# An encoder layer in fp32 on one core: attention's side work in other slots, the gate/up stage opened in another order, the last columns staggered

## The chip, the cores and the metric

The kernel runs on one core of a Trainium2 chip. The core has a matrix engine (TensorE, PE in the profile), a vector engine (VectorE, DVE), a scalar engine (ScalarE, ACT), a general engine (GpSimd, POOL) and a sync engine (SyncE, SP), which here issues the transfers. Each engine works through its own queue in order. The metric is device time of one launch in microseconds; less is better.

## The reference

One layer of an encoder on a 2048 x 1024 fp32 sequence: three kinds of mixing side by side, an output projection, and a gated feed-forward block.

```python
h = ada_norm(x, norm1_g, sh1, sc1)
proj = h @ w_in
y_na   = neighbourhood_attention(q, k, v, rpb)          # 4 heads, 2-D windows
y_mla  = latent_attention(c_q, c_kv, k_rope, ...)       # 8 heads, all 2048 keys
y_conv = short_conv(x_in, gate_b, gate_c, conv_w, conv_b)
mixed = concatenate([y_na, y_mla, y_conv], -1)
mixed = rms_norm(mixed in groups of 64, out_norm_g)
x = x + g1 * (mixed @ w_out)
h2 = ada_norm(x, norm2_g, sh2, sc2)
gt, up = split(h2 @ w_gu)                               # 1024 -> 2 x 2816
x = x + g2 * ((silu(gt) * up) @ w_down)                 # 2816 -> 1024
```

## The kernel before, in words

All arithmetic is fp32. A product is made of three passes over rounded halves (high x high, high x low, low x high; helper `three`), so each operand is split into a high part (a copy on ScalarE, `whl` or `put`) and a low part (a subtraction on VectorE). Work runs on 128-partition tiles and chunks of 512 tokens (CH).

**Latent attention** (lines 1030 to 1290) has 32 units, `mla`: 8 heads, each with 4 query chunks (qc). A unit has 8 key pairs, done two at a time: the loop steps through kp = 0, 2, 4, 6, and n counts key pairs over all units. For a key pair TensorE makes scores (L1198 to L1200), ScalarE the exponentials, GpSimd and VectorE add them into two running sums `acc` (L1212, L1213), and TensorE multiplies by the values (L1147), two key pairs later. The PE, ACT, DVE and POOL orders of this part are those of the code, since it stands in a hand-ordered section; SP's order is made by the scheduler. What is left of a unit is done in the slots of the next one:

- `finish` copies the result out of PSUM (L1155), and a DMA brings its upper half beside the lower (`o<-o`, L1157). `join` (L1159 to L1163) adds the halves on GpSimd (L1162) and stores them to `mixT`. It stands at kp = 2.
- `sums` closes the running sum in five stages, at kp = 0, 2, 2, 4, 4: GpSimd adds the two sums (L1175); ScalarE rounds the result (`ah`, L1178); GpSimd makes the rest (`al`, L1181); TensorE sums both over partitions with a vector of ones (L1184, L1185); ScalarE squares, and SP stores to `s2d` (L1188, L1189). For the last unit the first three stages are left out, and TensorE sums `acc` itself in full fp32 (L1173).
- `put_max` sends the next unit's row of maxima to its query tile (`qh<-mr`, L1141), which its first score product reads.
- `load_head` loads the next head's keys, queries and values, in the first unit of a head.
- `wd_combos` (L1034 to L1056) prepares differences of blocks of w_down: loads of four blocks (`wt`, L1044), four subtractions on GpSimd (L1054), each stored (`wdt`, L1056). It is a generator, stepped once each time n is a multiple of 4, five steps per set of blocks.

In attention's last units `mix_in(0)` prepares the first chunk for the projection, one step per call.

**Output projection** (`out_proj`, four chunks, two halves each): eight slices of w_out, each split by L1320 (ACT) and L1321 (DVE), then 12 matmuls (L1420 to L1422). Its `side` is a list of generators that are stepped once for each slice. Results are multiplied by a gate (L1455), added to x on GpSimd (L1456) and stored to `x1d` (L1428); in the last two chunks x is held in the four `xs` buffers.

**Gate and up.** A fast matrix product with seven products in place of eight, on 2 x 2 blocks: token blocks A11, A12, A22 and sums S1 to S4, against weight blocks B11 to B22 and sums T1 to T4 (made by L1346 on GpSimd from raw loads `draw`, L1334). `gate_set` does seven products of 12 matmuls (L1601 to L1603) in the order A11, S2, A12, S3, S1, A22, S4, and copies or adds their results (L1608 to L1629). `gate_up` runs one set for the gate, then one for up, for each of 11 column blocks f and each of two pairs of token chunks p. `first_early` and `first_late` make the token operands of the first pair (`put`, L1523 and L1524): `first_late` all of S3, S1, A22, S4 ahead of the first gate set. A22 takes the place of h1, which is why its four tiles are copied to `xs` buffers first (L1549). A list of units with a look-ahead of four gives the order in which weights are split; loads run up to three ahead.

**Down** (`down`): seven products over 11 slices of 2 x 512 rows, four token tiles each in its own PSUM bank; results go through VectorE (L1695, L1701) and GpSimd (L1703) to `out`. From `out_proj` on, PE and SP are in the order of the code; ACT, DVE and POOL by the scheduler.

## Time and profile before

| what | value |
|---|---|
| three runs | 3131.87, 3136.46, 3139.70 us (median 3136.46) |
| profiled execution | 3138.71 us, of it span 3136.9 us |
| PE busy | 2958.9 us (94%), mean granted clock 0.976 |
| VectorE, ScalarE, GpSimd busy | 2031.2, 1300.0, 1377.5 us |
| latent attention, 32 units | about 770 to 1558 us |
| output projection | 1566 to 1774 us |
| gate and up, down (first pair) | 1774 to 2487 us |
| gate and up, down (second pair) | 2487 to 3137 us |

In the rows below a line of the timeline holds the start, the length, the engine, the line of the code, the operation, output<-input by the program's names and shapes, and in brackets how long the engine sat idle before it and what released it. "x4" is four such instructions in a row, with the length of all. PEclk is the granted clock of TensorE, 1.00 being 2.4 GHz; its other level is half of that. A matmul's length is longer than its share of the engine's time, since matmuls overlap: at full clock one of 512 columns begins 0.23 us after the one ahead of it.

### The profile page before, as it was taken

Reading aid. Unit: us, or ns where it says so; the run is one execution under the profiler, and the core shown is the slowest. Engines: PE = TensorE matmul, PEld = TensorE weight load, DVE = VectorE, ACT = ScalarE, POOL = GpSimd, SP = SyncE. Lnnn points to the kernel's source line nnn. Section 1 sums busy time; section 2 is a strip of 40 time slices with the busy share of each in tenths; the row PEclk is TensorE's granted clock in tenths of the full one; section 3 lists DMA queues with packets and bytes.
Section 4 is the critical chain, followed back from the end, with each engine's and each line's share of the span. In section 5 each row is a group of like instructions: output and inputs, shape, how many; then the busy total and the mean of one; then the engine's idle time right before and its main releaser. Section 6 shows DMA issues by size and latency. Waiting matters only on the chain.

```text
span 3136.9 us, 38944 instructions
## 1 busy us (share of the span) xinstructions
PE 2958.9 (94%) x13554; PEld 2225.1 (71%) x13554; DVE 2031.2 (65%) x2892; ACT 1300.0 (41%) x2298; POOL 1377.5 (44%) x1011
## 2 busy tenths in 40 slices
PE   6988999889999999999999789999999899999998
PEld 5877788756555555555477567888777788888886
DVE  7778684646766676667666765665677655555556
ACT  4544454465433343334535433333354333333443
POOL 4433333432566666566645654445212344443002
PEclk9999999989999999999999899999999999999999
DMA  6566555786233322330255334333466633333565
GB/s 217 168 228 217 197 191 155 225 192 170 74 94 95 89 75 62 94 88 29 73 185 185 118 97 128 124 124 111 135 221 222 195 101 101 102 107 102 195 233 193
DMA packets 329575, 448.05 MB, mean 143 GB/s; under 512 B 39625, under 2 KB 178169, under 8 KB 326297
## 3 DMA queue, kind: packets, MB, share of 16 engines
q1 hardware_dynamic: 329378, 445.56, 46.0%
q8 instruction: 107, 1.75, 0.2%
q14 instruction: 90, 0.74, 0.1%
HBM read 323.70 MB, written 117.51 MB: 141 GB/s over the span
## 4 chain that ended last, share of the span: by engine, by line
PE 66%; DMA 11%; DVE 11%; issue 5%; POOL 3%; ACT 2%; SPq 1%; POOLq 0%; ACTq 0%; DVEq 0%
PE bk L1601 8%; PE bk L1603 8%; PE bk L1602 8%; PE op L1147 7%; PE ps L846 4%; PE bk L1421 3%; PE bk L1420 3%; PE bk L1422 3%; PE st L1198 3%; PE st L1199 3%; PE st L1200 3%; DVE whl L1321 2%; PE mm L316 2%; PE mm L320 2%; PE mm L321 2%
## 5 line engine op out<-in xcount | busy, mean ns | idle before, releaser
L847 DVE TENSOR_REDUCE mx<-ps 128x1 f32<-128x1024 f32 x256 | 313.0, 1223 | 251.6 <-PE ps L846 248.9
L1205 ACT ACTIVATE p<-st 128x1024 f32<-128x1024 f32 x256 | 261.8, 1023 | 405.9 <-PE st L1200 389.3
L1321 DVE TENSOR_TENSOR whl<-draw,whl 128x512 fp32r<-128x512 f32 x372 | 282.3, 792 | 183.7 <-ACT whl L1320 183.1
L1320 ACT ACTIVATE whl<-draw 128x512 fp32r<-128x512 f32 x372 | 219.3, 625 | 314.0 <-PE bk L1422 193.2
L1212 POOL TENSOR_TENSOR acc<-acc,p 128x512 f32<-128x512 f32 x192 | 256.6, 1336 | 122.7 <-ACT p L1205 118.9
L1421 PE MATMUL bk<-whl 128*128 128x512 f32 x616 | 243.5, 395 | 20.2 <-DVE whl L1321 20.2
L1147 PE MATMUL op<-p,vt 128*64 128x512 f32 x1024 | 253.5, 616 | 0.1
L1346 POOL TENSOR_TENSOR t<-draw 128x512 f32<-128x512 f32 x88 | 124.3, 1413 | 273.1 <-DMA draw<-in_w_gu 209.2
L1422 PE MATMUL bk<-whl 128*128 128x512 f32 x616 | 241.0, 391 | 0.0
L1420 PE MATMUL bk<-whl 128*128 128x512 f32 x616 | 240.8, 391 | 0.0
L1601 PE MATMUL bk<-q,whl 128*128 128x512 f32 x528 | 210.7, 399 | 24.5 <-ACT ev L1608 16.2
L1360 ACT ACTIVATE whl<-t 128x512 fp32r<-128x512 f32 x176 | 110.9, 631 | 274.8 <-PE bk L1603 238.5
L1361 DVE TENSOR_TENSOR whl<-t,whl 128x512 fp32r<-128x512 f32 x176 | 171.2, 974 | 62.8 <-ACT whl L1360 58.3
L1602 PE MATMUL bk<-q,whl 128*128 128x512 f32 x528 | 208.6, 395 | 0.0
L1603 PE MATMUL bk<-q,whl 128*128 128x512 f32 x528 | 207.7, 393 | 0.0
L1198 PE MATMUL st<-qh,kh 97*128 97x512 f32 x512 | 207.2, 405 | 0.0
L1199 PE MATMUL st<-ql,kh 96*128 96x512 f32 x512 | 204.1, 399 | 0.0
L1200 PE MATMUL st<-qh,kl 96*128 96x512 f32 x512 | 203.1, 397 | 0.0
L262 POOL TENSOR_TENSOR wlo<-raw,whi 128x768 fp32r<-128x768 f32 (+4 forms) x59 | 111.7, 1893 | 194.9 <-ACT whi L261 174.8
L1213 DVE TENSOR_TENSOR acc<-acc,p 128x512 f32<-128x512 f32 x192 | 193.1, 1006 | 4.3 <-ACT p L1205 4.2
L846 PE MATMUL ps<-kh,qh 96*128 96x512 f32 x512 | 179.2, 432 | 3.9 <-DMA kh<-krh 2.1
L320 PE MATMUL mm<-whi,hh 128*128 128x288 f32 (+3 forms) x512 | 171.4, 346 | 8.3 <-ACT hh L384 4.9
(353 smaller groups left out, 7269.0 us busy)
## 6 DMA issues: line engine op xcount, KB each, us to landing
draw<-in_w_gu SPq DMA_DIRECT2D x176, 256.0 KB
draw<-actd SPq DMA_DIRECT2D x70, 512.0 KB
actd<-xs SPq DMA_DIRECT2D x88, 256.0 KB
draw<-wdt SPq DMA_DIRECT2D x40, 512.0 KB
actd<-ev SPq DMA_DIRECT2D x66, 256.0 KB
wt<-in_w_adat SPq DMA_DIRECT2D x32, 512.0 KB
draw<-in_w_out SPq DMA_DIRECT2D x32, 512.0 KB
draw<-in_w_down SPq DMA_DIRECT2D x30, 512.0 KB
```

The costliest lines, as they stand in the source:

```text
L846: pe.matmul(ps[:, e], qs, kh[:QKD, kc:kc + CH], start=True, stop=True)
L847: v.reduce_max(mx[:, t, i:i + 1], ps.rearrange("p a b -> p (a b)"), axis=AX.X)
L1147: pe.matmul(tl["op"][e * HD:(e + 1) * HD], vt[:, 2 * kp + e], tl["p"][kp][:, e], start=kp == 0, stop=kp == NP - 1, skip_group_check=True)
L1198: pe.matmul(st[:, e], kh[:, ks], qh[:, qsl], start=True, stop=False)
L1199: pe.matmul(st[:, e], kh[:QKD, ks], ql[:, qsl], start=False, stop=False)
L1321: v.tensor_tensor(out=w[:, 1], in0=raw[:, e], in1=w[:, 0].bitcast(F32), op=ALU.subtract)
L1420: pe.matmul(ps, th, wh, start=first, stop=False, skip_group_check=True)
L1421: pe.matmul(ps, th, wl, start=False, stop=False, skip_group_check=True)
L1422: pe.matmul(ps, tl, wh, start=False, stop=last, skip_group_check=True)
L1601: pe.matmul(ps, w[:, 0, k], th, start=first and k == 0, stop=False, skip_group_check=True)
L1602: pe.matmul(ps, w[:, 0, k], tl, start=False, stop=False, skip_group_check=True)
L1603: pe.matmul(ps, w[:, 1, k], th, start=False, stop=k == KH - 1, skip_group_check=True)
```

## The change

Seven edits:

1. `join` goes from kp = 2 to kp = 4; in GpSimd's order it then stands behind `al` and two more additions.
2. `wd_combos` is stepped at kp = 4 and kp = 6 of every unit from n = 16 on, and its first yield of each set is gone, so a set takes four steps. It ends some six units earlier.
3. `mix_in(0)` gets one more step at the start of the last unit but one.
4. The last unit's sums leave attention: `last_sums` does them as a side generator of `out_proj(0)`, after its first two slices have been issued. `acp` moves to another pool group so that `acc` lives on.
5. For the first column block of the first pair the products go: gate A11, S2, A12; up A11, S2, A12; then the other four of gate, and the other four of up. The list of weight units follows, `first_late` becomes a generator that is stepped in between, and its copies to `xs` move from VectorE to ScalarE. The second half of the norm (`norm2_later`) starts with the second block, f = 1.
6. In `down`, for the last output block, `u2` is multiplied by the gate and added to x before its last product, so that only the product itself is multiplied and added behind it. Of these last additions GpSimd does those of token tiles 0 and 2, VectorE those of 1 and 3.
7. In the second pair's last product the last two slices are done token tile by token tile.

```diff
 wd_combos:
             for k in range(NFF // 2):
-                yield
                 if k + 1 < NFF // 2:
...
-                if n >= 16 and n % 4 == 0:
+                if n >= 16 and kp >= 4:
                     next(combos, None)
-                if prev and kp == 2:
+                if prev and kp == 4:
                     join(prev, state[prev])
...
+                if ui == len(mla) - 2 and kp == 0:
+                    next(side)
...
+            if f or p:
+                for u in range(2):
+                    item(2, partial(gate_load, f, u), gate_prep, 7)
+            else:
+                for u in range(2):
+                    item(2, partial(gate_load, f, u), gate_prep, 0)
+                i = len(stream) - 2
+                units.extend((i + u, e) for es in (range(3), range(3, 7)) for u in range(2) for e in es)
...
+    def last_sums(acc, u):
+        yield
+        sp = bank()
+        for e in range(2):
+            pe.matmul(sp[:1], ones_f[:, 0:1], acc[:, e], start=e == 0, stop=e == 1)
+        t = tmp()
+        s.activation(t[:1], sp[:1], AF.Square, scale=math.sqrt(EPS))
+        dma(s2d[u[0]:u[0] + 1, u[1] * CH:(u[1] + 1) * CH], t[:1])
...
 first_late:
             put(S, "S3", k, t)
+            yield
...
-            v.tensor_copy(t, h1[:, KH + k])
+            s.activation(t, h1[:, KH + k], AF.Copy)
...
 gate_up:
-        gate_set(S, gate, side)
+        sets = [gate_set(S, gate, side, f + p == 0), gate_set(S, up, side, f + p == 0)]
+        if f + p == 0:
+            next(sets[0])
+            next(sets[1])
+            drain(early)
+        for _ in sets[0]:
+            pass
         stores()
-        gate_set(S, up, side)
+        for _ in sets[1]:
+            pass
...
 down, prod:
+                if end and k == NK - 2:
+                    held = a, w
+                    continue
+                ks = ((k - 1, *held), (k, a, w)) if end and k == NK - 1 else ((k, a, w),)
...
+                        if (i, j) == (0, 1):
+                            v.tensor_tensor(out=u2[t], in0=u2[t], in1=g2b[:, CH:], op=ALU.mult)
+                            g.tensor_tensor(out=xx, in0=xx, in1=u2[t], op=ALU.add)
...
-        prod(c, False, (0, 1))
-        add(u2, u2, c)
-        put_out(0, 1, u2)
+        prod(c, False, (0, 1), p == PAIRS - 1)
+        put_out(0, 1, c)
```

The lines of the changed kernel have other numbers: L1175, L1181, L1162, L1212 and L1054 become L1170, L1176, L1161, L1207 and L1053; L1334 and L1428 become L1332 and L1432; L1695 and L1701 become L1734 and L1740, L1703 becomes L1742.

GpSimd's order around one end of a unit in attention: `acc` are the score sums and, in the row with one input, the close of the unit's sum; `o` is `join`, `al` the rest of the rounded sum, `wt` a weight sum. Before:

```order
L1212 TENSOR_TENSOR acc<-acc,p_9184 128x512
L1175 TENSOR_TENSOR acc<-acc 128x512
L1212 TENSOR_TENSOR acc<-p_9195,p_9222 128x512
L1212 TENSOR_TENSOR acc<-acc,p_9238 128x512
L1162 TENSOR_TENSOR o_9209<-o_9209,o 64x512
L1181 TENSOR_TENSOR al<-acc,ah 128x512
L1212 TENSOR_TENSOR acc<-acc,p_9264 128x512
L1212 TENSOR_TENSOR acc<-acc,p_9284 128x512
L1054 TENSOR_TENSOR wt<-wt 128x512
```

And after:

```order
L1207 TENSOR_TENSOR acc<-acc,p_8840 128x512
L1170 TENSOR_TENSOR acc<-acc 128x512
L1207 TENSOR_TENSOR acc<-p_8853,p_8880 128x512
L1207 TENSOR_TENSOR acc<-acc,p_8892 128x512
L1176 TENSOR_TENSOR al<-acc,ah 128x512
L1207 TENSOR_TENSOR acc<-acc,p_8918 128x512
L1207 TENSOR_TENSOR acc<-acc,p_8936 128x512
L1053 TENSOR_TENSOR wt<-wt 128x512
L1161 TENSOR_TENSOR o_8867<-o_8867,o 64x512
```

`join` has moved from ahead of `al` to three operations behind it, past a weight sum.

SP's order at the opening of the gate stage: `draw<-in_w_gu` are gate and up weights (four loads make one column block of gate or up), `x1d<-xs` the last stores of the projection, `n<-x1d` loads for the norm, `actd` stores of the first block's results. Before:

```order
L1428 DMA x1d<-xs 128x512 x4
L1446 DMA xs<-in_x 128x512 x4
L1334 DMA draw<-in_w_gu 128x4x128 x8
L1495 DMA n_15653<-x1d 128x512
L1428 DMA x1d<-xs 128x512 x4
L1428 DMA h2d<-n_15736 128x4x128
L1334 DMA draw<-in_w_gu 128x4x128 x4
L1495 DMA n_15807<-x1d 128x512
```

And after:

```order
L1432 DMA x1d<-xs 128x512 x4
L1460 DMA xs<-in_x 128x512 x4
L1332 DMA draw<-in_w_gu 128x4x128 x12
L1432 DMA x1d<-xs 128x512 x4
L1332 DMA draw<-in_w_gu 128x4x128 x4
L1509 DMA n_15936<-x1d 128x512
L1432 DMA actd<-ev 128x512 x2
```

Twelve weight loads stand ahead of the last `x1d` stores, where eight stood, and the norm's first load comes behind them.

VectorE's last operations: `u` are the four token tiles of the last output block, `bk` their PSUM banks, `g2b` the gate, `xs` the tiles that are stored. Before:

```order
L1695 TENSOR_TENSOR u_23928<-u_23928,bk 128x512
L1695 TENSOR_TENSOR u_23929<-u_23929,bk 128x512
L1701 TENSOR_TENSOR u_23928<-u_23928,g2b 128x512
L1695 TENSOR_TENSOR u_23930<-u_23930,bk 128x512
L1701 TENSOR_TENSOR u_23929<-u_23929,g2b 128x512
L1695 TENSOR_TENSOR u_23931<-u_23931,bk 128x512
L1701 TENSOR_TENSOR u_23930<-u_23930,g2b 128x512
L1701 TENSOR_TENSOR u_23931<-u_23931,g2b 128x512
```

And after:

```order
L1740 TENSOR_TENSOR u_23932<-bk,g2b 128x512
L1740 TENSOR_TENSOR u_23933<-bk,g2b 128x512
L1742 TENSOR_TENSOR xs<-xs,u_23933 128x512
L1740 TENSOR_TENSOR u_23934<-bk,g2b 128x512
L1740 TENSOR_TENSOR u_23935<-bk,g2b 128x512
L1742 TENSOR_TENSOR xs<-xs,u_23935 128x512
```

The four additions from PSUM are gone, the multiplication reads PSUM itself, and two sums with x are now here.

## Rows read from the trace of the kernel before

**Rows 1.** The page's chain that ended last, shares by engine.

```profile
PE 66%; DMA 11%; DVE 11%; issue 5%; POOL 3%; ACT 2%; SPq 1%; POOLq 0%; ACTq 0%; DVEq 0%
```

**Rows 2.** PE's waits: what waited, for whom, us in total, times, longest.

```profile
PE bk L1601 <- ACT ev L1608: 16.2, 1, 16.2
...
PE mi L1185 <- POOL al L1181: 15.1, 6, 2.8
...
PE bk L1601 <- DVE ev L1618: 6.0, 1, 6.0
PE bk L1420 <- ACT whl L1320: 5.6, 2, 3.9
```

**Rows 3.** Windows of a head's first unit, its second, and six heads.

```profile
core 0: us, PE busy (x) PEld busy (x) DVE busy (x) ACT busy (x) POOL busy (x), PEclk, DMA share, GB/s
864.01:891.71 27.70, 25.50 (x100) 14.38 (x99) 17.38 (x19) 9.81 (x11) 15.93 (x12) 0.94 0.85 188
891.71:915.47 23.76, 23.76 (x100) 13.91 (x99) 16.49 (x19) 9.69 (x11) 15.15 (x11) 1.00 0.08 25
864.01:1461.18 597.17, 582.03 (x2378) 337.48 (x2377) 404.28 (x410) 233.34 (x264) 375.21 (x278) 0.98 0.32 80
```

**Rows 4.** Timeline of POOL in those two units.

```profile
881.02 1.27 POOL L1162 TENSOR_TENSOR o<-o,o 64x512 f32<-64x512 f32 x1 [7.14 <-DMA o<-o]
882.26 1.78 POOL L1181 TENSOR_TENSOR al<-acc,ah 128x512 fp32r<-128x512 f32 x1
...
905.16 1.27 POOL L1181 TENSOR_TENSOR al<-acc,ah 128x512 fp32r<-128x512 f32 x1 [1.88 <-ACT ah L1178]
```

**Rows 5.** Timeline of SP, ACT and PE at that head change.

```profile
868.65 0.49 SPq L1157 DMA_DIRECT2D o<-o  x1
...
876.76 0.62 ACT L1178 ACTIVATE ah<-acc 128x512 fp32r<-128x512 f32 x1
...
884.09 0.40 PE L1185 MATMUL mi<-al,ones_r 128*1 128x512 f32 x1 [2.20 <-POOL al L1181]
```

**Rows 6.** Timeline from attention to the projection: SP, PE, ACT, PE.

```profile
1554.86 0.90 SPq L1069 DMA_DIRECT2D m<-mixT  x2
...
1555.42 2.22 PE L1147 MATMUL op<-p,vt 128*64 128x512 f32 x8
...
1562.36 2.17 ACT L1090 ACTIVATE t<-m 128x512 f32<-128x512 f32 x4
...
1566.15 0.79 PE L1420 MATMUL bk<-whl,th 128*128 128x512 f32 x1 [3.94 <-ACT whl L1320]
```

**Rows 7.** Window of the first gate/up block, same columns as rows 3.

```profile
1774.50:1850.30 75.80, 47.62 (x177) 36.42 (x177) 59.45 (x57) 30.77 (x57) 62.45 (x41) 0.82 0.25 74
```

**Rows 8.** Timeline of SP, POOL and ACT in that block.

```profile
1785.96 11.49 SPq L1428 DMA_DIRECT2D x1d<-xs  x4
...
1793.72 3.38 POOL L1456 TENSOR_TENSOR xs<-xs,eg 128x512 f32<-128x512 f32 x2
...
1797.89 0.60 ACT L1608 ACTIVATE ev<-bk 128x512 f32<-128x512 f32 x1
...
1812.34 6.75 POOL L1555 TENSOR_TENSOR ev<-ev,tl 128x512 f32<-128x512 f32 x4
```

**Rows 9.** Timeline of DVE near attention's end, one operation.

```profile
1543.82 3.70 DVE L1124 TENSOR_TENSOR tl<-t,th 128x512 fp32r<-128x512 f32 x1 [0.98 <-ACT th L1123]
```

**Rows 10.** Timeline of DVE in the second pair's down stage.

```profile
2978.30 1.29 DVE L1321 TENSOR_TENSOR whl<-draw,whl 128x512 fp32r<-128x512 f32 x2 [1.43 <-ACT whl L1320]
```

**Rows 11.** Timeline of PE at the second pair's first gate block.

```profile
2491.29 0.79 PE L1601 MATMUL bk<-m,whl 128*128 128x512 f32 x1 [4.26 <-DVE ev L1612]
```

**Rows 12.** Timeline of the end: PE, DVE, POOL.

```profile
3126.87 0.39 PE L1422 MATMUL bk<-whl 128*128 128x512 f32 x1
...
3129.69 2.03 DVE L1701 TENSOR_TENSOR u<-u,g2b 128x512 f32<-128x512 f32 x2
...
3131.25 2.81 POOL L1703 TENSOR_TENSOR xs<-xs,u 128x512 f32<-128x512 f32 x2 [0.68 <-DVE u L1701]
```

**Rows 13.** Timeline of SP at the head change: one weight load.

```profile
873.83 7.92 SPq L1044 DMA_DIRECT2D wt<-in_w_down  x1
```

More of the change, by code (lines that the diff above doesn't have):

```diff
@@ L1006, in encoder_trunk @@
         egp = c5.enter_context(tc.tile_pool(name="egp", bufs=2, reuse_waits="tile"))
+        acp = c5.enter_context(tc.tile_pool(name="acp", bufs=2, reuse_waits="tile"))
         pw = mk("pw", 6)
-        acp = mk("acp", 2)
         ms = mk("ms", 1)
@@ L1167, in sums @@
             acc = tl["acc"]
-            if u == mla[-1] and stage < 3:
+            if u == mla[-1]:
                 pass
-            elif u == mla[-1] and stage == 3:
-                tl["sp"] = pmi.tile([P, CH], F32, name="mi")
-                for e in range(2):
-                    pe.matmul(tl["sp"][:1], ones_f[:, 0:1], acc[:, e], start=e == 0, stop=e == 1)
             elif stage == 0:
@@ L1274, in encoder_trunk @@
                             if stage == 4:
+                                last_acc = state[prev]["acc"]
                                 del state[prev]
@@ L1377, in encoder_trunk @@
         for f in range(NK):
-            for u in range(2):
-                item(2, partial(gate_load, f, u), gate_prep, 7)
+            if f or p:
[6 more added lines that the diff above has]
+                units.extend((i + u, e) for es in (range(3), range(3, 7)) for u in range(2) for e in es)
         for op, name in zip(LEFT, ORDER):
@@ L1541, in first_late @@
             put(S, "S3", k, t)
+            yield
+        a22, s4 = [], []
+        s2 = hi_lo(S, "S2").bitcast(F32)
         for k in range(KH):
@@ L1545, in first_late @@
             put(S, "S1", k, t)
-        a22, s4 = [], []
-        for k in range(KH):
             t = xsp.tile([P, CH], F32, name="xs")
-            v.tensor_copy(t, h1[:, KH + k])
+            s.activation(t, h1[:, KH + k], AF.Copy)
             a22.append(t)
-        s2 = hi_lo(S, "S2").bitcast(F32)
-        for k in range(KH):
             t = ev.tile([P, CH], F32, name="ev")
@@ L1556, in first_late @@
             s4.append(t)
+            yield
         for k in range(KH):
             put(S, "A22", k, a22[k])
+            if k % 2:
+                yield
         for k in range(KH):
             put(S, "S4", k, s4[k])
+            if k % 2:
+                yield
     def operands(p, S):
@@ L1591, in operands, with gate_set @@
                 yield
-    def gate_set(S, after, side):
+    def gate_set(S, after, side, lead):
         def prod(ps, op, first):
@@ L1606, in gate_set @@
         prod(a, "A11", True)
+        if lead:
+            step(side, 2)
         p1 = ev.tile([P, CH], F32, name="ev")
@@ L1612, in gate_set @@
         v.tensor_tensor(out=u2, in0=p1, in1=b, op=ALU.add)
-        step(side)
+        step(side, 2 if lead else 1)
         prod(a, "A12", False)
         after(0, 0, a)
+        if lead:
+            step(side, 2)
+        yield
         prod(b, "S3", False)
@@ L1675, in down, with prod @@
         xs = []
-        def prod(ps, first, at=None):
+        def prod(ps, first, at=None, end=False):
             for k in range(NK):
                 a, w = unit_next(), unit_next()
+                if end and k == NK - 2:
+                    held = a, w
+                    continue
+                ks = ((k - 1, *held), (k, a, w)) if end and k == NK - 1 else ((k, a, w),)
                 for t in range(NTT):
                     sl = slice(t * P, (t + 1) * P)
-                    three(ps[t], a[:, 0, sl], a[:, 1, sl], w[:, 0], w[:, 1], first and k == 0, k == NK - 1)
+                    for kk, a, w in ks:
+                        three(ps[t], a[:, 0, sl], a[:, 1, sl], w[:, 0], w[:, 1], first and kk == 0, kk == NK - 1)
                 if k == 4:
@@ L1699, in put_out @@
             for t in range(NTT):
-                e = u3[t] if src is a else src[t]
+                e = u3[t] if src is a else u2[t] if src is c else src[t]
                 v.tensor_tensor(out=e, in0=src[t], in1=gb, op=ALU.mult)
                 xx = xs.pop(0)
-                g.tensor_tensor(out=xx, in0=xx, in1=e, op=ALU.add)
+                (v if src is c and t % 2 else g).tensor_tensor(out=xx, in0=xx, in1=e, op=ALU.add)
                 pending.append((out[tokens(2 * p + i, t), j * CH:(j + 1) * CH], xx))
+        c = None
         a = four()
@@ L1738, in encoder_trunk @@
         x1a = block("q0").rearrange("p (t h) n -> p t (h n)", h=2)
-        out_proj(0, mTs[0], [mix(1)], x1a)
+        out_proj(0, mTs[0], [last_sums(last_acc, mla[-1]), mix(1)], x1a)
         x1b = block("q1").rearrange("p (t h) n -> p t (h n)", h=2)
@@ L1753, in encoder_trunk @@
                     side = [norm2_later()]
-                    first_late(S, h0, h1)
+                    early = [first_late(S, h0, h1)]
                 for f in range(NK):
-                    gate_up(p, f, S, side)
+                    gate_up(p, f, S, early if f + p == 0 else side)
                 drain(side)
```

## The prediction

> **What bounds the kernel now.** I began with the page's chain of waits. TensorE (PE) makes 66% of the chain that ended last, and no other engine more than 11% [rows 1], so only what shortens PE's own path counts: its idle stretches, the stretches after them in which it runs at half clock, and what comes behind its last matmul. The profiled execution took 3138.71 us, 2.25 above the median of 3136.46; the sum below is made against it. Second I read PE's waits. Four groups of them are met by this change: 15.1 us in six pieces for `al`, 16.2 for the copy of the first gate product, 6.0 for L1618, and 5.6 for w_out splits, the largest 3.9 [rows 2]. What each is worth is read from its own stretch, because the slow clock behind a gap costs as much again.
>
> **Attention: `al` no longer behind `join`.** The windows give 23.76 us, PE never idle, for a unit inside a head, and 27.70 us for the second head's first unit, where PE is busy 25.50 with the same 100 matmuls: 2.20 idle and 1.74 through the clock, 0.94 granted as a mean of the two levels. The six heads from 864.01 to 1461.18 take 597.17 us; 24 units of 23.76 would be 570.2, so the head changes lose 27.0 [rows 3]. The cause is on GpSimd: `join` (L1162) sat idle 7.14 us for its half-tile copy, and `al` (L1181) stood behind it until 882.26. Inside a head `al` waits 1.88, for ScalarE's `ah` alone [rows 4]. The copy was issued at 868.65, behind the next head's loads; `ah` was ready at 876.76 + 0.62 = 877.4; PE wanted `al` at 884.09 - 2.20 = 881.9 [rows 5]. In the changed order `al` is the next thing on GpSimd after two score sums, so it ends near 877.4 + 1.3 = 878.7, 3 us before PE asks. `join` comes two sums later, after 881, when its copy has landed; nothing on PE waits for it, only its store to mixT. So -27. The weak end is the idle time alone without the slow clock, -15; the strong end is the whole, -28. I take -27, since both parts are in these windows and the mean unit without the wait stands beside them. The weight sums (L1054) are 1.3 us of GpSimd each, 44 calls in place of 55 for the same 44 subtractions; GpSimd is busy 15.15 of a unit's 23.76 [rows 3], so their new slots cost nothing as long as SP's queue flows (a rival below).
>
> **Handover to the output projection.** Before, attention's last value products end at 1555.42 + 2.22 = 1557.64, and PE's first projection product starts at 1566.15 after an idle 3.94; ahead of the split that it waits for, ScalarE did the square of the sum and four L1090 copies (2.17 us) [rows 6]. Up to 1562.2 PE had only the sum's matmuls and one broadcast, and another wait. Now the two sum matmuls come after the first two of the eight weight slices, and two L1090 copies are left ahead of the first split. The loads that L1090 waits for are issued from 1554.86 [rows 6] and land, as I estimate, 4.5 us later, near 1559.4; then two copies (1.1) and the split: product at about 1561.3, 4.8 us earlier. The sum matmuls come back as four passes of 0.24 (23.76 us for 100 matmuls, [rows 3]). With the clock still falling in the shorter gap I take -4; bounds -1 (the gap only changes its name) and -7 (all idle and all slow clock gone).
>
> **Gate opening.** The stretch from 1774.50 to 1850.30 is 75.80 us with PE busy 47.62, clock 0.82 [rows 7]: up to 28 us of idle and slow clock lie here, and the new order of products (three of gate, three of up, then the rest) is made for that. I do not expect most of it, and this is the step I am least sure of. (1) The copy of the first product started on ScalarE at 1797.89, behind squares that wait for GpSimd's residual sums, the last of which run from 1793.72 [rows 8]. It is still behind them after the change. GpSimd loses the four S1 sums ahead of it (6.2 us) and gains two weight combinations (3.0), so the copy starts some 3 us earlier, and A12 can go from about 1795.6. (2) The six products and S3, S1 then fill PE to about 1815. (3) A22 overwrites a buffer of h1, after copies (now ScalarE's, L1565) into `xs` buffers that the last x1d stores must leave. Those stores waited 11.49 us over four issues from 1785.96 [rows 8]; now SP issues twelve gate loads ahead of them in place of eight, and the last four of these (unit f=1) wait until the T4 combination and its split have freed raw buffers. GpSimd's 22 operations up to T4, at 1.6 us each from 1775, and the two of the norm end near 1812; split, load issue, stores and an estimated 2.3 us of flight bring the copies to about 1824 and A22 to 1826.5. PE waits about 11.5 and then runs two products at half clock. (4) A22 5.2, S4 2.8, four more up-products 11.2: f=1 starts at about 1846, against 1850.3. So -4; bounds -20 (A22 is there when PE comes) and +7 (GpSimd late).
>
> One rule bears here. The S4 operands on GpSimd took 6.75 us for four [rows 8], 1.69 each, against 1.27 for the one at 881.02 [rows 4]; both take two tiles, but VectorE worked on two-tile operands beside the slower ones. So 22 operations cost between 28 and 37 us, and my 1.6 sits high in it. The Trainium skill ("SBUF — State Buffer", "SBUF: two separate sides") says that VectorE with two SBUF inputs and a GpSimd operation that reads SBUF exclude each other for a whole instruction. By that rule T4 would come some 2 us later, and the opening would gain 2 instead of 4. The trace agrees in kind: a VectorE subtraction of this shape took 3.70 us at 1543.82 beside three GpSimd operations in a row [rows 9], against 0.65 alone [rows 10].
>
> **Second pair's gate start.** PE waited 4.26 us at 2491.29 for L1612 on VectorE [rows 11], queued behind eight operations of the last output block (four additions from PSUM, four multiplications). Now the four multiplications of `u2` come a product earlier, the additions are gone into the sums with x, and two of the four GpSimd sums go to VectorE: net two fewer on VectorE, 0.65 each alone and 1.0 beside GpSimd's sums (2.03 for two, [rows 12]), and two fewer on GpSimd, 1.3 to 1.7 each, ahead of the out stores behind which SP holds gate loads. Idle and half clock together, I take -5, bounds -2 and -8.
>
> **Early `u2` multiplications.** Four per pair, on VectorE among the splits of w_down. There it idles 1.43 us before a pair of splits of 1.29 [rows 10]; 4 x 0.65 = 2.6 fit in two such idle times, but the order puts them together, so a split may be 1.2 late while three prepared slices cover it. +1, bounds 0 and +3.
>
> **Tail.** PE's last matmul ends at 3126.87 + 0.39 = 3127.26. VectorE goes on until 3131.72, GpSimd's last sums until 3131.25 + 2.81 = 3134.06 [rows 12], and the span ends 2.84 later with the last store. Now the last product finishes token tile by token tile (two slices of three matmuls, 1.4 us apart), and behind each stand one multiplication from PSUM (0.7 to 1.0) and one addition, the fourth on VectorE (0.65 to 0.7). Last addition near 3129.2: -4.8, bounds -3 (one GpSimd operation of 1.26 in the way) and -5.5. The last product now needs its last two weight slices at once, where a VectorE split ended little before its use; that may take 1 back, and is in the weak bound.
>
> **Sum.** -27 - 4 - 4 - 5 + 1 - 4.8 = -43.8, or 3138.7 - 43.8 = 3094.9 on the profiled execution and 3092.7 against the median. I give 3094.
>
> **Rivals.** (a) Attention gives only its idle time (-15): the clock falls at the head change for another reason, for instance because the head's loads delay something else. Against it: inside heads the clock is 1.00 with the same loads of weights. It gives 3092.7 + 12 = 3105; chance 0.10. (b) The gate opening works: A22 is ready when PE arrives, because the raw buffers come free before T4. The gain there is 20 in place of 4, so 3077 to 3083, say 3080; chance 0.14. For it: GpSimd at 1.27 an operation would end T4 by 1803. (c) The gate opening stalls longer: f=1's gate loads ahead of the x1d stores hold `xs` past 1833; with it products at half clock, +7 for -4: 3104; chance 0.12. (d) Slower. SP's queue in attention: a `wt` load must wait for the store of an earlier sum, and with both sums at kp 4 and 6 the load can stand ahead of the row of maxima that the next unit's first score product needs. At the second head's first unit SP already stood 7.92 us at such a load from 873.83 [rows 13], to 881.75, and the next unit began at 891.71, so some 7 to 9 us of room remain. If 22 units each lost 3 us (2.0 idle and 1.0 clock), +66 less 44: 3158. It decides from a delay of about 10 us of that queue in every unit; chance 0.03. (e) The change doesn't do what it says, and `al` is as late as before: against it stands the order of GpSimd shown above. With the rest it gives 3120; chance 0.03, a part of it without the rest.
>
> **How the numbers follow.** Forecast 0.58 (3085 to 3101), (b) 0.14, (c) 0.12, (a) 0.10, (d) 0.03, (e) 0.03. A measurement can tell 0.3%, 9.4 us, from no change. All but (d) and that part of (e) are faster by more: faster 0.95, within 0.02, slower 0.03. The range takes the forecast, (b), (c) and (a) with the unknown ends: 3076 to 3112.
>
> **What would show it.** Right: no PE wait for `al` at head changes, 23.8 us for each head's first unit, clock 1.00 there; first projection product within 4 us after the last value product; PE still waits once, about 10 us, for an A22 operand near 1815 to 1827; last addition 2 us behind the last matmul. Wrong: a score product waiting for `qh`; no A22 wait at all (b); f=1 of the gate later than 1850 less what was gained before (c); half clock at head changes without a gap (a).

## The result

The changed kernel takes 3098.9 us (median of four runs, 3096.71 to 3102.54), against 3136.49 for the kernel before: ratio 0.9882, 95% interval 0.9865 to 0.9900. In a second set of five runs it took 3102.68 against 3131.34: 0.9907 (0.9894 to 0.9920). The forecast was 3094, with a range of 3076 to 3112. The direction, the size and the range hold. Of the six terms of the sum, two hold (attention and the tail), the three other gains came out at half or less in the first profile, and the one cost was twice its size. Some 10 us of the difference between the two profiled executions lie ahead of attention, where the code is the same, as the stages show.

Both traces can be cut at the same matmuls: first score product, last value product, first projection product, first gate product and so on. Each stage is the difference of two such starts on PE's timeline; only the last value product and the last matmul count by their ends, and the last stage ends with the span.

| stage | before | changed | changed, second set | forecast of the difference |
|---|---|---|---|---|
| up to attention (code not touched) | 769.97 | 759.58 | 758.91 | 0 |
| attention | 787.67 | 760.91 | 762.46 | -27 |
| last value product to first projection product | 8.50 | 4.23 | 4.23 | -4 together |
| output projection | 208.36 | 210.80 | 209.84 | with the row above |
| first gate/up block | 75.79 | 74.74 | 75.14 | -4 |
| ten other blocks, first pair | 395.32 | 396.59 | 397.20 | 0 |
| first down stage | 232.88 | 235.30 | 234.05 | +1 with the second |
| second pair's first block | 48.12 | 45.63 | 45.97 | -5 |
| its ten other blocks | 385.07 | 385.07 | 385.07 | 0 |
| second down stage | 215.57 | 217.67 | 217.06 | see above |
| behind the last matmul | 9.67 | 4.43 | 4.42 | -4.8 |

From attention on the changed kernel is 31.6 us shorter (2366.96 to 2335.36; 2335.43 in the second set). The other 10.4 us of the two profiled executions lie ahead of attention, where PE, ACT, DVE, POOL and SP have the same instructions in the same order; over all fourteen profiles taken here that first part lies between 758.9 and 770.0, and the profile of before has the longest. The first down stage scatters too: 229.2, 232.9 and 235.8 in three kernels with the down stage of before, so its +2.4 says nothing.

PE's waits in the changed kernel, the same view as [rows 2]; the lines have the new numbers (L1629 is the copy of the first gate product, L1537 and L1538 are the high and low halves of `put`):

```profile
PE bk L1620 <- ACT ev L1629: 13.7, 2, 13.5
...
PE bk L1620 <- ACT q L1537: 9.5, 1, 9.5
PE bk L1424 <- ACT whl L1318: 5.9, 4, 4.2
...
PE bk L1621 <- DVE q L1538: 5.3, 1, 5.3
```

The 15.1 us for `al` are gone from the list. The 16.2 for the first product's copy is 13.5 now, and where 6.0 stood for L1618 there are 9.5 and 5.3 for A22's halves. The windows that answer to [rows 3 and 7]: the second head's first unit, the same six heads, and the first gate/up block.

```profile
853.63:877.38 23.75, 23.75 (x101) 13.90 (x99) 17.30 (x19) 9.70 (x11) 16.33 (x13) 1.00 0.98 219
853.63:1423.70 570.07, 570.07 (x2377) 333.73 (x2376) 412.81 (x410) 232.85 (x264) 383.11 (x282) 1.00 0.36 89
...
1735.51:1810.25 74.74, 45.37 (x168) 34.96 (x169) 52.58 (x51) 29.42 (x53) 60.49 (x40) 0.77 0.23 68
```

A head's first unit now takes what any other takes, PE is never idle in six heads, and the clock is 1.00. GpSimd at that head change, as in [rows 4], shows why:

```profile
867.07 1.28 POOL L1176 TENSOR_TENSOR al<-acc,ah 128x512 fp32r<-128x512 f32 x1 [3.57 <-ACT ah L1173]
868.30 2.96 POOL L1207 TENSOR_TENSOR acc<-acc,p 128x512 f32<-128x512 f32 x2
871.23 1.77 POOL L1053 TENSOR_TENSOR wt<-wt 128x512 f32<-128x512 f32 x1
872.97 1.27 POOL L1161 TENSOR_TENSOR o<-o,o 64x512 f32<-64x512 f32 x1
```

`al` waits for ScalarE alone and ends at 868.35; `join` starts 4.6 us after that, without a wait for its copy.

### The profile page after: what moved, and what is told of

Same layout as the page of the kernel before. It is cut to its first block, busy times and chain, and to the rows that moved or that the text cites. A ratio compares the mean times of both kernels' runs of the same rounds, so it can differ in the third digit from the quotient of the medians.

```text
span 3094.9 us, 38942 instructions
## 1 busy us (share of the span) xinstructions
PE 2937.3 (95%) x13554; PEld 2211.7 (71%) x13554; DVE 2039.2 (66%) x2892; ACT 1302.2 (42%) x2302; POOL 1387.4 (45%) x1015
## 3 DMA queue, kind: packets, MB, share of 16 engines
q8 instruction: 107, 1.75, 0.2%
## 4 chain that ended last, share of the span: by engine, by line
PE 71%; DVE 11%; DMA 8%; issue 4%; POOL 3%; ACT 2%; SPq 1%; POOLq 0%; DVEq 0%; ACTq 0%
PE bk L1620 8%; PE bk L1622 8%; PE bk L1621 8%; PE op L1146 7%; PE ps L846 5%; PE st L1193 4%; PE bk L1425 4%; PE st L1194 4%; PE bk L1424 4%; PE st L1195 4%; PE bk L1426 4%; DVE whl L1319 2%; PE mm L316 2%; PE mm L320 2%; PE mm L321 2%
## 5 line engine op out<-in xcount | busy, mean ns | idle before, releaser
L1207 POOL TENSOR_TENSOR acc<-acc,p 128x512 f32<-128x512 f32 x192 | 265.4, 1382 | 51.4 <-ACT p L1200 46.8
L1424 PE MATMUL bk<-whl 128*128 128x512 f32 x616 | 240.8, 391 | 0.5 <-ACT whl L1318 0.4
L1208 DVE TENSOR_TENSOR acc<-acc,p 128x512 f32<-128x512 f32 x192 | 201.6, 1050 | 3.9 <-ACT p L1200 3.7
```

Source lines behind the costliest of these rows:

```text
L1424: pe.matmul(ps, th, wh, start=first, stop=False, skip_group_check=True)
```

## The experiments

Each is told with its edit, what was on record before it ran, and what came out. Totals of single executions differ by the part ahead of attention, so stages are compared.

**Only `join`.** The kernel before with this edit:

```diff
-                if prev and kp == 2:
+                if prev and kp == 4:
                     join(prev, state[prev])
```

> The kernel before with one edit: join at kp = 4 in place of 2; the weight sums stay in their slots. Theory (al stood behind join on GpSimd, and the half clock came from that gap): no PE wait for al, every head's first unit 23.8 us, the six heads 570 us, 27 less than before, total about 3109. Rival (the clock falls at a head change for another reason): only the idle 15 go, total about 3121. Rival (the new slots of the weight sums are needed too): a wait for al of 1 us or more stays at head changes.

Measured: 3101.74 us (four runs, 3101.05 to 3102.22), ratio 0.9893 (0.9868 to 0.9918). The six heads:

```profile
858.04:1428.10 570.06, 570.06 (x2378) 333.72 (x2377) 404.14 (x409) 232.61 (x264) 378.09 (x279) 1.00 0.34 85
```

Attention takes 760.95 us, as in the changed kernel. So this one line is 26.7 of the 31.6 us, idle time and half clock both, and the rivals fall. That the total is lower than expected comes from the part ahead of attention (764.0) and a short first down stage (229.2). From attention on this kernel takes 2336.44 us, 1.1 more than the changed one, with a first down stage that is 5 to 6 us shorter; by their ratios (0.9893 here, 0.9882 and 0.9907 for the whole change) the two kernels can't be told apart.

**Only the weight sums.**

```diff
             for k in range(NFF // 2):
-                yield
                 if k + 1 < NFF // 2:
...
-                if n >= 16 and n % 4 == 0:
+                if n >= 16 and kp >= 4:
                     next(combos, None)
```

> The kernel before with the weight sums at kp = 4 and 6 and without the extra yield; join stays at kp = 2. Theory: the waits for al stay at 15 us in six pieces, within 2 us, and no score product waits for qh, so 3136 within noise. Rival (GpSimd's crowding by weight sums made al late): the waits shrink by half or more. Rival (SP's queue holds qh behind the weight loads): units longer than 23.8 us inside heads, total above 3150.

Measured: 3147.74 us (one run), attention 795.41, 7.7 longer than before. No unit inside a head is longer than 23.76; all of it is at the head changes. PE's wait, and GpSimd at the second head:

```profile
PE mi L1184 <- POOL al L1180: 20.3, 6, 4.3
```

```profile
878.17 1.25 POOL L1161 TENSOR_TENSOR o<-o,o 64x512 f32<-64x512 f32 x1 [8.99 <-DMA o<-o]
```

The theory was that the waits stay, the rival that they shrink. They grew by 5.2 us, since `join`'s copy came later still in SP's queue: at the six head changes it was issued 5.1 to 5.7 us into the unit, where it was 4.6 to 4.9 before (at the second head eight of the head's loads stand ahead of it, seven before). So alone this edit costs; with `join` out of the way nothing is left of the cost. The place of SP's transfers was the hidden half of this edit.

**The handover undone.** The changed kernel with the last unit's sums in attention again.

```diff
-            if u == mla[-1]:
-                pass
+            if u == mla[-1] and stage < 3:
+                pass
+            elif u == mla[-1] and stage == 3:
+                tl["sp"] = pmi.tile([P, CH], F32, name="mi")
+                for e in range(2):
+                    pe.matmul(tl["sp"][:1], ones_f[:, 0:1], acc[:, e], start=e == 0, stop=e == 1)
...
-        out_proj(0, mTs[0], [last_sums(last_acc, mla[-1]), mix(1)], x1a)
+        out_proj(0, mTs[0], [mix(1)], x1a)
```

> The changed kernel with the last unit's sums back in attention's last slot, in full fp32 ahead of the projection; everything else as changed. Theory (moving them saves the first product 4.3 us, but brings back two fp32 matmuls of 1.9 us and a late second split of 0.9 inside the first eight weight slices): from the last value product to the first projection product 8.5 us in place of 4.2, the first half of the first chunk 27.6 in place of 30.2, total about 1.7 more than the changed kernel. Rival (the slow clock in the shorter gap costs the 2.6): the first half stays at 30.

Measured: 3102.19 us (one run). From the last value product to the first projection product 9.24 us (4.23 in the changed kernel), the projection 207.26 (210.80 and 209.84), together 216.50 against 215.03 and 214.07. The ten profiles with the sums moved have 214.1 to 215.5 for the two together, so the move is worth 1.0 to 2.4 us, on one run without it, and the theory holds: what the first product gains is mostly paid behind it. In the changed kernel PE shows the payment:

```profile
1524.72 0.79 PE L1424 MATMUL bk<-whl,th 128*128 128x512 f32 x1 [4.22 <-ACT whl L1318]
1526.38 0.80 PE L1425 MATMUL bk<-whl,th 128*128 128x512 f32 x1 [0.87 <-DVE whl L1319]
...
1533.76 1.88 PE L1442 MATMUL bk<-acc,ones_f 128*1 128x512 f32 x4
```

**The gate opening undone.** The changed kernel with all seven products of the gate, then all of up, and `first_late` as it was:

```diff
-        sets = [gate_set(S, gate, side, f + p == 0), gate_set(S, up, side, f + p == 0)]
-        if f + p == 0:
-            next(sets[0])
-            next(sets[1])
-            drain(early)
+        sets = [gate_set(S, gate, side, False), gate_set(S, up, side, False)]
...
```

> The changed kernel with the gate stage opened as before (all seven products of gate, then all of up; first_late in one go, copies on VectorE; the norm from the first block on). Theory (the new opening trades one wait for another and moves the norm's transposes to later blocks): the first block 75 to 78 us, all 11 blocks of the first pair 470 to 472 us as in the changed kernel, so total within 2 us of it. Rival (the opening gains what was forecast): 474 or more, total 4 more.

Measured: 3102.41 us (one run). The first block takes 75.67 us, the 11 blocks 470.89, against 471.33 and 472.34 in the changed kernel (471.11 before). The new opening gains nothing: 1 us in its block, given back in the later ones, which now hold the norm's transposes. From attention on this run is all the same 2.5 us longer than the changed kernel (2337.82 to 2335.36), since its second down stage took 220.33 us (217.67 and 217.06): PE waited 1.93 us for a split at the staggered end and then ran at half clock. Nothing in that stage was edited, so it is counted as scatter here.

**The x1d stores ahead of the next loads.** The changed kernel with one line more:

```diff
         if f + p == 0:
             next(sets[0])
+            stores()
             next(sets[1])
             drain(early)
```

> The changed kernel with the last x1d stores issued by SP ahead of the gate loads of f = 1, not behind them. Theory (A22 waits because SP holds those stores behind loads that wait for raw buffers): the 14.8 us of waits at A22 go; S4, whose operands GpSimd finishes 5 us after A22 is wanted, waits some 5 us instead; f = 1 starts about 10 us earlier than in the changed kernel, total about 3089. Rival (GpSimd's chain itself makes A22 late): A22 still waits 10 us or more and the total stays near 3099.

Measured: 3095.3 us (four runs), ratio 0.9872 (0.9842 to 0.9902). The first block takes 70.63 us: 4.1 less, not 10. A22's waits of 9.5 and 5.3 are gone, so SP's queue was the cause of them; but PE still waits 0.61 us for a weight split on ScalarE, 3.64 for one on VectorE, and 1.47 and 0.73 for the low halves of S4 there. PE's idle time in the block fell by 7.7 us, and 3.6 of that came back as PE busy for the same products (45.37 us in the changed kernel, 48.96 here), since more of them ran at half clock. VectorE and GpSimd in that stretch:

```profile
1785.13 1.76 DVE L1359 TENSOR_TENSOR whl<-draw,whl 128x512 fp32r<-128x512 f32 x1
1786.81 1.76 DVE L1538 TENSOR_TENSOR q<-ev,q 128x512 fp32r<-128x512 f32 x1
1788.50 0.67 DVE L1646 TENSOR_TENSOR ev<-ev,bk 128x512 f32<-128x512 f32 x1
```

```profile
1784.62 1.72 POOL L1344 TENSOR_TENSOR t<-draw,t 128x512 f32<-128x512 f32 x1
1786.30 1.73 POOL L1344 TENSOR_TENSOR t<-draw 128x512 f32<-128x512 f32 x1
1788.11 1.61 POOL L1344 TENSOR_TENSOR t<-draw,t 128x512 f32<-128x512 f32 x1
```

An operation with two tiles from SBUF takes VectorE 1.76 here, and GpSimd 1.72. The records overlap, but their ends alternate: GpSimd's at 1786.34, VectorE's at 1786.89, GpSimd's at 1788.03, VectorE's at 1788.57, GpSimd's at 1789.72. The VectorE operation whose second input is a PSUM bank (L1646) takes 0.67. The Trainium skill ("SBUF — State Buffer", "SBUF: two separate sides") has this as an exclusive lock: of a VectorE operation with two SBUF inputs and a GpSimd operation that reads SBUF, the one that starts first holds it for the whole instruction. The alternating ends and the 0.67 with a PSUM input agree with it.

**Four products ahead of A12.** On top of that, gate A11, S2 and up A11, S2, and only then A12 of both.

```diff
-                units.extend((i + u, e) for es in (range(3), range(3, 7)) for u in range(2) for e in es)
+                units.extend((i + u, e) for es in (range(2), (2,), range(3, 7)) for u in range(2) for e in es)
...
         step(side, 2 if lead else 1)
+        if lead:
+            yield
         prod(a, "A12", False)
...
```

> The kernel with early x1d stores (the run e3_sp), and four products ahead of A12: gate A11, S2, up A11, S2, then A12 of both. PE then has 5.6 us of work in the idle 14 us before A12. Theory (the wait that ends last in this block is for GpSimd's S4 and T4 behind it, and for VectorE's splits): the idle comes back before A22 and S4, the block stays within 2 us of e3_sp's 70.6. Rival (every idle us saved at A12 counts): the block is 5 us or more shorter.

Measured: 3096.91 us (four runs), ratio 0.9885 (0.9855 to 0.9915); the block 70.63 us, the same as without. The wait before A12 falls from 14.0 to 7.75, and what was saved comes back as 4.0 in four pieces for S1's halves, 5.92 for a weight split and 3.16 for VectorE's L1644. As the theory had it, what ends last is behind A12.

**S3 and S1 on VectorE.** On top of the early stores, the eight sums of `first_late` that make S3 and S1:

```diff
-            g.tensor_tensor(out=t, in0=h0[:, k], in1=h1[:, k], op=ALU.subtract)
+            v.tensor_tensor(out=t, in0=h0[:, k], in1=h1[:, k], op=ALU.subtract)
...
-            g.tensor_tensor(out=t, in0=h1[:, k], in1=h1[:, KH + k], op=ALU.add)
+            v.tensor_tensor(out=t, in0=h1[:, k], in1=h1[:, KH + k], op=ALU.add)
```

> The kernel with early x1d stores (the run e3_sp), and the eight sums of S3 and S1 on VectorE in place of GpSimd; GpSimd keeps S4, the weight combinations and the sums with x. Theory (a two-tile operation of VectorE and one of GpSimd exclude each other, so 8 times 1.3 us on GpSimd is more of the shared time than 8 times 0.65 on VectorE): the squares ahead of the first product's copy end 5 us earlier, S4 is ready some 10 us earlier, VectorE's splits near A22 take 0.7 to 1.2 in place of 1.75; the block 58 to 63 us in place of 70.6, total about 3086. Rival (VectorE is the bound here and gets eight more operations): the block no shorter than 69.

Measured: 3091.72 us (four runs, 3089.85 to 3096.33), ratio 0.9875 (0.9839 to 0.9911). The time is the lowest of all; the ratio is not (0.9872 with the early stores alone), so by totals the two can't be told apart, and the block is compared. The block with early stores, and with this:

```profile
1739.05:1809.68 70.63, 48.96 (x169) 36.59 (x169) 53.82 (x51) 28.89 (x53) 60.99 (x40) 0.78 0.24 73
```

```profile
1739.00:1803.13 64.13, 44.61 (x169) 34.09 (x169) 59.60 (x59) 28.87 (x53) 49.14 (x32) 0.84 0.26 79
```

Eight operations moved: GpSimd is busy 11.85 us less, VectorE 5.78 more, and the block 6.5 shorter, 1 us short of the theory's range. Of the 6.5, 2.15 are idle time and 4.35 are PE busy (48.96 to 44.61), that is, fewer products at half clock. The rival falls, but of the theory's signs only a part came: the squares ahead of the first product's copy did not end earlier (PE waits 13.60 at A12 still), GpSimd's last operation for S4 ends 46.0 us into the block (45.6 without the edit), and VectorE's splits near A22 take 1.2 us in some places and 1.76 to 1.78 in others. What did move is the last sum for S1. With the early stores alone, GpSimd does it behind four subtractions for S4, and VectorE's low halves of A22 stand behind it:

```profile
1773.68 1.30 POOL L1562 TENSOR_TENSOR t<-q 128x512 f32<-128x512 f32 x1
```

```profile
1776.70 3.48 DVE L1538 TENSOR_TENSOR q<-xs,q 128x512 fp32r<-128x512 f32 x2
```

With S3 and S1 on VectorE:

```profile
1763.88 0.68 DVE L1562 TENSOR_TENSOR t<-q 128x512 f32<-128x512 f32 x1
...
1766.79 6.89 DVE L1538 TENSOR_TENSOR q<-xs,q 128x512 fp32r<-128x512 f32 x4
```

The sum ends 25.6 us into the block in place of 35.9, and the low halves begin at 27.8 in place of 37.7. So the place in GpSimd's queue explains the gain at least as well as the time that the two engines take from each other; no run here separates the two.

**S4 on VectorE too, and the early sums sooner.** The run above, with S4's eight subtractions on VectorE and with x loaded at the sixth weight slice in place of the eighth. Beside it the last edit alone in the changed kernel, and both together with four products ahead of A12.

```diff
-            g.tensor_tensor(out=t, in0=h0[:, KH + k], in1=s2[:, 0, k], op=ALU.subtract)
-            g.tensor_tensor(out=t, in0=t, in1=s2[:, 1, k], op=ALU.subtract)
+            v.tensor_tensor(out=t, in0=h0[:, KH + k], in1=s2[:, 0, k], op=ALU.subtract)
+            v.tensor_tensor(out=t, in0=t, in1=s2[:, 1, k], op=ALU.subtract)
...
-                if k == 7 and at:
+                if k == (5 if at == (0, 1) else 7) and at:
```

> The changed kernel with x loaded and summed into u2 two weight slices earlier in the last product of each pair (at the sixth slice in place of the eighth). Theory (the four early sums on GpSimd, 1.7 us each, slow VectorE's last four splits to 1.45 us each, and the staggered end waits 1.4 for them): the last down stage 215.2 us in place of 217.7, the tail still 4.4 behind the last matmul. Rival (the staggered end itself, or the multiplications of u2, cost the 2.1): the last down stage stays at 217 or more.

> The run e8_port with the eight subtractions of S4 on VectorE too, and the earlier sums of e9_k5. Theory (what GpSimd does beside VectorE is paid by both): the first block 59 to 62 us in place of 64.1, last down stage 215, total about 3087. Rival (VectorE, 59.6 us busy of 64.1 in e8_port, is now the bound): the block 64 or more; then the total is that of e8_port less the 2 us of the end, about 3090.

> The run e10_s4 with four products ahead of A12, as in e7_four. Theory (with GpSimd's chain shortened, the idle before A12 is on the path again): the first block 3 to 6 us shorter than in e10_s4. Rival (VectorE's splits end last whatever the order of products): within 1.5 us of e10_s4.

Measured: 3104.26 us (one run), 3099.19 (four runs, ratio 0.9893, 0.9878 to 0.9909) and 3103.98 (four runs, 0.9910, 0.9897 to 0.9924). The first block takes 65.2 us with S4 moved and 64.4 with four products first, against 64.1: the block is in the rivals' range both times, and moving more to VectorE gains nothing. VectorE is busy 57.5 us of the 65.2, less than the 59.6 above with eight operations fewer, since most of its operations now take 0.68; but PE waits 6.14 us for L1642, so VectorE's queue now ends last. With the sooner sums the second down stage is 222.3, 221.9 and 221.0 us, longer than in any other run (217.0 to 220.3 in the seven with the early `u2` and x loaded as in the changed kernel). By the number that is the rival's side, but for a reason that neither side had; the totals expected for the second and third run were missed for it too. The first down stage is longer too, 240.8 to 241.8 us (229.2 to 236.7 in the eleven other profiles), and the second pair's first block is shorter, 41.4 to 42.5 (45.6 to 46.3 in those seven). SP, ScalarE and PE near the end of the first of the three show a new wait:

```profile
3078.16 2.29 SPq L1725 DMA_DIRECT2D xs<-x1d  x4
3080.51 0.42 SPq L1032 DMA_DIRECT2D draw<-in_w_down  x1
```

```profile
3086.82 2.71 ACT L1318 ACTIVATE whl<-draw 128x512 fp32r<-128x512 f32 x5 [7.92 <-DMA draw<-in_w_down]
```

```profile
3087.50 0.50 PE L1424 MATMUL bk<-whl 128*128 128x512 f32 x1 [3.84 <-ACT whl L1318]
```

The loads of x need the buffers that the stores of the block ahead leave; SP stood at them until 3078.16, and the last two weight loads, which the staggered end needs at once, went out behind, 204.8 and 205.7 us into the stage. In the changed kernel only the last one is behind the loads of x, and the two go out at 199.1 and 204.7.

**The early `u2` undone.** The changed kernel without the early multiplication and sum, and with all four last sums with x on GpSimd; the end is still staggered.

```diff
-                        if (i, j) == (0, 1):
-                            v.tensor_tensor(out=u2[t], in0=u2[t], in1=g2b[:, CH:], op=ALU.mult)
-                            g.tensor_tensor(out=xx, in0=xx, in1=u2[t], op=ALU.add)
...
-        put_out(0, 1, c)
+        add(u2, u2, c)
+        put_out(0, 1, u2)
```

> The changed kernel without the early multiplications of u2 and without VectorE's part in the last sums; the last product is still staggered. Theory (four multiplications in a row delay the weight splits of down): the two down stages are 2.4 and 2.1 us shorter again; the second pair's first gate block loses its 2.5; after the last matmul an addition, a multiplication and a GpSimd sum remain, about 1 us more than in the changed kernel; total within 2 us of it. Rival (the down stages are longer for another reason, by chance or by the stagger): they stay as long as in the changed kernel.

Measured: 3104.55 us (one run). The second down stage is 215.03 (217.67 and 217.06 with the early part), the second pair's first block 47.93 (45.63 and 45.97), the time behind the last matmul 7.51 (4.43). The first down stage did not get shorter, so of the theory's 2.4 there nothing is left. The stagger alone is thus worth 2.2 us of the end (9.67 to 7.51), the early part with VectorE's two sums another 3.1 and some 2 in the second pair's first block, less 2.0 to 2.6 in the second down stage (1.9 to 5.3 over the seven profiles, 217.0 to 220.3). What costs there are not the multiplications, which VectorE did from 2933.6 to 2938.5. VectorE and GpSimd in the changed kernel:

```profile
3079.24 6.39 DVE L1319 TENSOR_TENSOR whl<-draw,whl 128x512 fp32r<-128x512 f32 x5 [2.64 <-ACT whl L1318]
```

```profile
3079.98 6.79 POOL L1729 TENSOR_TENSOR xs<-xs,u 128x512 f32<-128x512 f32 x4 [13.63 <-DMA xs<-x1d]
```

The last five splits take 1.28 us each beside GpSimd's four sums, and PE waits 1.41 for the last of them at 3085.68; without the sums in that place five such splits took 3.10 (in the run with the sooner sums, from 3087.48), and PE's wait at the stagger is 0.23 in the run without the early part. No run took the sums out and left the multiplications, so this rests on the rows.

**The changed kernel again**, beside these on one chip.

> The changed kernel again, beside the others on one chip. Its stages repeat within 1 us from attention on, but for the first down stage (3 us); the time up to attention varies by some 5 us from run to run, as in all runs here. Ratio to the kernel before 0.987 to 0.990.

Measured: 3102.68 us (five runs, 3096.13 to 3105.22), ratio 0.9907 (0.9894 to 0.9920): above the expected ratio, with the kernel before at 3131.34 there. The stages stand in the table of the result; the largest difference from the first profile is 1.5 us, in attention's first unit, where 1 was expected. Ahead of attention the fourteen profiles lie 11 us apart, not 5.

## Why the prediction was right, and where it was not

1. *Attention, -27.* Right in place, mechanism and size: 26.8 us, and the one line of `join` alone gives 26.7. The idle time was 15.1, so 12 us of it were the half clock behind the gaps, as the windows of [rows 3] had it. `al` ended 3.0 us before PE took it (868.35 and 871.34), the 3 us of the forecast.
2. *Handover, -4.* Half. The first product did come 4.3 us earlier (4.8 was worked out), but the projection got 2.4 longer in that trace. The step that failed is the price of the sum's matmuls: four passes of 0.24 were taken, and the four records of L1442 took 1.88 us, at full clock, twice that. The trace of before had this price, in the same two products at their old place:

```profile
1559.91 1.88 PE L1173 MATMUL mi<-acc,ones_f 128*1 128x512 f32 x4 [2.26 <-POOL acc L1212]
```

And the second split, 0.87 late, was not in the sum.

3. *Gate opening, -4.* The walk was right where it was most detailed: the copy came 2.7 us earlier in its block (forecast 3), PE reached A22 at 40.7 us after the block's first product (forecast 40.5), and A22's first copy waited for the x1d stores, which SP issued behind the gate loads. Wrong was the size of the last step: 14.8 us at A22 in place of 11.5. The copies came 45.7 us into the block, 3.8 sooner than worked out, but VectorE stood between A22's high and low halves with splits that took 1.75 beside GpSimd, and the low half cost a second wait. And 1.3 us came back in the later blocks, which the sum did not have. Net zero (the opening undone: 470.9 against 471.3 for the 11 blocks). Rival (b), a gain of 20, did not come even with two edits more, the stores earlier and S3 and S1 on VectorE: the block is then 64.1, 11.7 less than before. SP, ScalarE and PE of the changed kernel at that place (the eight loads are the last of the twelve):

```profile
1731.46 46.17 SPq L1332 DMA_DIRECT2D draw<-in_w_gu  x8
1777.67 2.18 SPq L1432 DMA_DIRECT2D x1d<-xs  x4
```

```profile
1781.22 0.63 ACT L1565 ACTIVATE xs<-q 128x512 f32<-128x512 f32 x1 [1.12 <-DMA x1d<-xs]
```

```profile
1785.68 0.79 PE L1620 MATMUL bk<-q,whl 128*128 128x512 f32 x1 [9.46 <-ACT q L1537]
1791.77 0.80 PE L1621 MATMUL bk<-q,whl 128*128 128x512 f32 x1 [5.29 <-DVE q L1538]
```

4. *Second pair's start, -5.* 2.1 to 2.5. The term counted operations taken out of VectorE's and GpSimd's queues ahead of the wait for L1612; that wait (L1633 now) fell from 4.26 to 3.69 only, and the later one from 2.32 to 0.77. With x loaded two slices sooner the first of the two is gone and the block is 41.4 to 42.5 us, but the stage ahead is 5 to 8 us longer.
5. *Early `u2`, +1.* 2.1 and 1.5 us in the second down stage, by a mechanism that was not on the list: I priced the multiplications and not the four sums with x that were moved with them, onto the splits that the staggered end needs first. In the first down stage it can't be told from the scatter.
6. *Tail, -4.8.* 5.2, as worked out: in the changed kernel PE's last matmul ends at 3090.12 + 0.39 = 3090.51, and VectorE's last sum with x, which answers to GpSimd's last in [rows 12], 1.5 us later.

```profile
3090.12 0.39 PE L1426 MATMUL bk<-whl 128*128 128x512 f32 x1
```

```profile
3091.34 0.69 DVE L1742 TENSOR_TENSOR xs<-xs,u 128x512 f32<-128x512 f32 x1
```

7. *The sum.* Forecast -43.8, from attention on -31.6; without the first down stage -34.0. The sum was thus 12 us too large where it applies. The medians fell by 37.6 and 28.7 in two sets; that the first lies 5 us from the forecast is in part luck: in the part ahead of attention, which the sum put at nothing, the profile of before was the longest of fourteen. Whether the moved pool of `acc` has a share in that (kernels with the old place: 764.0 to 770.0 in three profiles, with the new one 758.9 to 769.2 in eleven) stays open.

Rival (d), a slower kernel by SP's queue, did not come, but the room was smaller than worked out: SP stood 9.01 us at a weight load at the second head and issued `qh` at 871.81, with the next unit at 877.38.

```profile
862.70 9.01 SPq L1044 DMA_DIRECT2D wt<-in_w_down  x1
871.81 0.66 SPq L1140 DMA_DIRECT2D qh<-mr  x1
```

No score product waited for it.

## What to carry to other kernels

Look for the short operation that stands behind a transfer in an in-order queue: one line moved here is worth more than the six other edits together, and it counts nearly double (15.1 us of waits, 26.7 gained), since the slow clock follows the gap. A change in the order of products pays only when all that feeds the late operands moves too; SP's queue, GpSimd's chain and VectorE's splits each took over in turn. When an operation is moved, price all that goes with it: what stands behind it in its old and its new queue, and what the engine next door is doing then.

## What the runs showed of the hardware

- VectorE and GpSimd slow each other, and the ends of their operations alternate: a subtraction of two 128x512 tiles on VectorE takes 0.68 us alone and 1.76 beside GpSimd, GpSimd's 1.27 alone and 1.73 beside VectorE, while VectorE with one input in PSUM keeps 0.67 (the run with the early stores).
- Two products of unsplit fp32, 128x512 against one column of ones, leave four records in the trace of 0.47 us each at full clock (1.88 in all, before and after), where a pass of the rounded halves begins 0.23 to 0.24 us after the one ahead; with a granted clock of 0.54 they took 3.41 (the run with the handover undone).
- One early load can cost more than a late one: with four loads two slices earlier the second down stage took 221.0 to 222.3 us in three runs, against 217.0 to 220.3 in seven, since SP stood at them with weight loads behind.
